# Norming delta-rule and attention outputs tile by tile, inside their loops, in a two-layer hybrid block

## The chip, the cores and the metric

The kernel runs on one core of a Trainium2 chip. The metric is the device time of one execution in microseconds (us). Engines are named PE (TensorE, matrix products), DVE (VectorE), ACT (ScalarE), POOL (GpSimd) and SP (SyncE, which here only issues transfers).

## The reference

Two layers work on 256 latent and 256 context tokens of width 1024. Each layer modulates its normed input, projects it with one wide matrix, runs three branches over the projections, gates and merges the three and applies a feed-forward part (a dense one in layer 0, eight experts with two per token in layer 1). In layer 1 only the latent tokens are needed after the branches, so its outputs are half as wide.

```python
# branch a: gated delta rule in chunks, both directions, 4 heads x 128
o = _rmsnorm(o.transpose(0, 2, 1, 3), gn) * jax.nn.silu(z.reshape(bsz, n, HA, DVA))
# branch b: gated linear attention in chunks, both directions, 4 heads x 128
o = _rmsnorm(o.transpose(0, 2, 1, 3), gn) * jax.nn.silu(r.reshape(bsz, n, HB, DVB))
# branch c: differential attention, 4 heads: softmax(q1 k1) - lam * softmax(q2 k2), times v
o = _rmsnorm(o, gn) * (1.0 - lam_init)
# merge of the three
(ga * (ya @ w_o_a) + gb * (yb @ w_o_b) + gd * (yd @ w_o_c)) @ w_out
```

Each branch's output is divided by its root mean square over the 128 values of a head and token, so a token's norm needs that token alone. The mean is over one head: heads are independent.

## The kernel before

**Layout.** A branch's output oT lies as 128 head values on the partitions by head by token: `oT[:, h, t]` (512 tokens in layer 0, 256 in layer 1). The sum of squares over the partitions is a matmul with a matrix of ones, which leaves the sum on every partition.

**Products.** A float32 projection is done as three matmuls (mm3, L272 to L274) of operands that are split in a high part (ACT copy, L267) and a rest (DVE subtraction, L268). Weights stream through three buffers named raw, filled from SP's queue in the order in which they are written.

**Order of work.** PLAN lists the stages of a layer: pr and iv prepare the delta rule's chunks and invert their triangular matrices, sc is `a_scan`, gla the linear attention, dif the `diff` attention, ha, hb and hc are `head_out` of the branches, ma, mb and mc their merges. "m16" asks for 16 units of the modulation matrices (w_mod; L348, a load of 1 MB and eight matmuls each, four units to a group), "ga4" for gate projections ahead of time, "za" for z's projection ahead of time, stored in DRAM and read again later. Within the program a list scheduler of the programming layer decides each engine's order: it lets later work run ahead of earlier work where that waits. Tiles of a pool, though, are handed out in the program's order. PSUM tiles come from two such pools, `pm` (tag "mm", 3 tiles: projections, modulation, merges, norms) and `pq` (tag "q", 5 tiles: the steps of scan and attention). Each engine then executes its list in order.

**The chains.** `a_scan` (L730) takes four steps, in each the two directions; a step's 128 tokens go through w (L746), V (L759, L761), sp (L767) and o (L781, L782), and the state S is carried to the next step. In the order table `[[0, 1, 2, 3], [1, 0, 3, 2]]` a tile of tokens is written by one direction (copy, L784) and completed by the other in an odd step (addition, L786). `diff` (L1039) takes query tiles of 128 tokens and in each the heads in turn: products pq (L1052), maximum (L1053), exponential (L1056), combination (L1061, L1062), transposes tp (L1065), copy PT (L1067) and products oc (L1069); after the four heads oc is copied to oT.

**The outputs.** `head_out` (L825) norms a branch's finished oT head by head over all its tokens: square (ACT, L842), ones matmul (L844), the inverse root (`rstd`, two ACT steps, L407), multiplications (DVE), split. For branch a it reads the stored z back whole into a raw buffer (`fetch`, L232).

Of the kernel before, what the change touches and what calls it, by code (L numbers as in the profile page):

```python
# [13 lines left out]
AF = mybir.ActivationFunctionType  # L14
OP = mybir.AluOpType
# [9 lines left out]
MOE_PART = 3  # L25
PRE = (7,)
PLAN = ("sm ap su pr iv ga4 m4 za sc m16 dec qkB gb1 ha ma vB gla qC kC m4 gc1 vC hb dif mb hc mc",
        "sm ap pr ga1 m8 iv sc za m6 ga3 m1 gc1 qkB dec vB ha ma gla qC kC m1 vC hb dif mb hc mc")
MOE_PRE = 9
MOE_AT = 0  # L30
PART = 512
# [165 lines left out]
class Prog:  # L197
# [532 lines left out]
    def a_scan(self, l, s):  # L730
        nc, D, T = self.nc, self.D, self.T
        t0 = 2 * l
        oT = self.ch([4, 512 - 256 * l], "oTa")
        mm = nc.tensor.matmul
        bc = lambda n, d, tt: D[n][:, d, tt][:, :, None].to_broadcast([128, 4, 128])
        S = [None, None]
        wT = {}
        order = [[0, 1, 2, 3], [1, 0, 3, 2]]

        def wt(i, d):  # L740
            tt = order[d][i]
            X = self.sm([4, 128], "Xs")
            nc.vector.tensor_mul(X, s["U"][d][:, 4 * tt:4 * tt + 4], bc("negc", d, tt))
            p = self.pq((4, 128), "w")
            for h in range(4):
                mm(p[:, h], s["k"][:, tt, h], X[:, h], start=True, stop=True)  # L746
            wT[d] = self.sm([4, 128], "wT")
            nc.scalar.copy(wT[d], p)

        for i in range(4):  # L750
            for d in range(2):
                tt = order[d][i]
                out = tt >= t0
                qs = slice((tt - t0) * 128, (tt - t0 + 1) * 128)
                if i:
                    wt(i, d)
                V = self.pq((4, 128), "V")
                for h in range(4):
                    mm(V[:, h], s["U"][d][:, 4 * tt + h], s["v"][:, tt, h], start=True, stop=not i)  # L759
                    if i:  # L760
                        mm(V[:, h], wT[d][:, h], S[d][:, h], start=False, stop=True)  # L761
                if i < 3:
                    vk = self.sm([4, 128], "vk")
                    nc.vector.tensor_mul(vk, V, bc("bk", d, tt))
                    sp = self.pq((4, 128), "sp")
                    for h in range(4):
                        mm(sp[:, h], s["k"][:, tt, h], vk[:, h], start=True, stop=True)  # L767
                if out:
                    vn = self.sm([4, 128], "vn")
                    nc.vector.tensor_mul(vn, V, bc("beta", d, tt))  # L770
                    if l:
                        qe = T["q"][:, 1 - d, :, qs]
                    elif i:
                        R = self.a_rows(d, tt)
                        qe = self.sm([4, 128], "qe")
                        nc.scalar.activation(qe, R, AF.Exp)
                        nc.vector.tensor_mul(qe, qe, T["q"][:, :, qs])
                    o = self.pq((4, 128), "o")
                    for h in range(4):
                        if i:  # L780
                            mm(o[:, h], S[d][:, h], qe[:, h], start=True, stop=False)  # L781
                        mm(o[:, h], vn[:, h], s["AT"][d][:, tt - t0, h], start=not i, stop=True)  # L782
                    if i % 2 == 0:
                        nc.scalar.copy(oT[:, :, qs], o)  # L784
                    else:
                        nc.vector.tensor_add(oT[:, :, qs], oT[:, :, qs], o)  # L786
                if i < 3:
                    Sn = self.sm([4, 128], "S")
                    if not i:
                        nc.scalar.copy(Sn, sp)  # L790
                    else:
                        for h in range(4):
                            nc.vector.scalar_tensor_tensor(Sn[:, h], S[d][:, h], D["egl"][:, d, tt, h:h + 1],
                                                           sp[:, h], op0=OP.mult, op1=OP.add)
                    S[d] = Sn
        return oT
# [14 lines left out]
    def gates_ahead(self, l, j, H, count):  # L811
# [5 lines left out]
        for _ in range(count):  # L817
            pr = len(done)
            done.append(pr)
            for c, p in enumerate(self.proj(l, U_G + 3 * pr + j, H, 256 * l)):  # L820
                s = self.sd([512], "sg")[:, :n]
                self.sigmoid(s, p)
                self.nc.scalar.dma_start(g[pr // 2][:, 2 * (pr % 2) + c], s)

    def head_out(self, l, oT, gn, H, u, name):  # L825

        nc = self.nc
        c0 = 256 * l
        n = 512 - c0
        zs = self.stashed.get((l, "z" + name))  # L830
        if l == 0:
            yh = self.ch([4, 512], "yh", F32R)
            yl = self.ch([4, 512], "yl", F32R)
        else:
            y = self.ch([2, 4, 256], "yhl", F32R)
            yh, yl = y[:, 0], y[:, 1]
        for h in range(4):
            o = oT[:, h]
            if zs is None and u is not None and h % 2 == 0:
                pz = self.proj(l, u + h // 2, H, c0)  # L840
            sq = self.sd([512], "sq")
            nc.scalar.activation(sq[:, :n], o, AF.Square)  # L842
            ps = self.pm()
            nc.tensor.matmul(ps[:, :n], self.ones, sq[:, :n], start=True, stop=True)  # L844
            if zs is not None:
                rs = self.rstd(ps[:, :n], n, 1.0 / 128)
                if h == 0:
                    z = self.fetch(zs)
                nc.vector.tensor_mul(o, o, rs[:, :n])
                nc.vector.tensor_mul(o, o, z[:, h])  # L850
            elif u is None:
                rs = self.rstd(ps[:, :n], n, 1.0 / 128)
                nc.vector.scalar_tensor_tensor(o, o, gn, rs[:, :n], op0=OP.mult, op1=OP.mult)
            else:

                pv = next(pz)
                z = self.sd([512], "z")
                nc.scalar.activation(z[:, :n], pv, AF.Exp, scale=-1.0)
                nc.vector.scalar_tensor_tensor(o, o, gn, pv, op0=OP.mult, op1=OP.mult)
                nc.scalar.activation(z[:, :n], z[:, :n], AF.Ln, bias=self.one)  # L860
                nc.scalar.activation(sq[:, :n], ps[:, :n], AF.Ln, bias=self.eps, scale=1.0 / 128)
                nc.vector.scalar_tensor_tensor(z[:, :n], sq[:, :n], 0.5, z[:, :n], op0=OP.mult, op1=OP.add)
                nc.scalar.activation(z[:, :n], z[:, :n], AF.Exp, scale=-1.0)
                nc.vector.tensor_mul(o, o, z[:, :n])
            self.split(yh[:, h], yl[:, h], o)
        if self.dbg is not None and f"{name}{l}" in self.dbg:
            nc.sync.dma_start(self.dbg[f"{name}{l}"][:, :, c0:512], oT)
        return yh, yl
# [170 lines left out]
    def diff(self, l, q, k, vC):  # L1039
        nc = self.nc  # L1040
        mm = nc.tensor.matmul
        oT = self.ch([4, 512 - 256 * l], "oTc")
        for qt in range(2 * l, 4):
            nk = 256 if qt < 2 else 512
            cs = slice((qt - 2 * l) * 128, (qt - 2 * l + 1) * 128)
            o = self.pq((4, 128), "oc")
            for h in range(4):
                E, r = [], self.ti([4], "r")
                for m in range(2):
                    ms = slice(64 * m, 64 * m + 64)  # L1050
                    p = self.pq()
# [16 lines left out]
                for j in range(nk // 128):  # L1068
                    mm(o[:, h], vC[:, j, h * 128:(h + 1) * 128], PT[:, j], start=j == 0, stop=j == nk // 128 - 1)  # L1069
            nc.scalar.copy(oT[:, :, cs], o)  # L1070
        return oT


# [499 lines left out]
```

## Time and profile before

| | |
|---|---|
| median of 3 runs | 2604.29 us |
| lowest and highest | 2601.22 and 2613.67 us |
| profiled execution | 2607.5 us, its span 2605.7 us |
| mean granted PE clock | 0.962 |
| PE busy | 2455.8 us (94% of the span) |
| DVE busy | 1718.3 us (66%) |
| ACT busy | 1417.3 us (54%) |
| HBM traffic | 181 GB/s over the span |

The profiled execution is a run of its own, so its times are compared with it and not with the median. A busy engine may be busy with work that could stand elsewhere; what sets a stage's length is read from that stage's windows and waits. In all times of the trace 0 is the start of the span.

### The profile page before, as it was taken

The numbers are of one execution on the slowest core, as the hardware profiler recorded it, in microseconds if no ns is written. First come the engines' busy times: TensorE is split into PE (matmuls) and PEld (weight loads), VectorE is DVE, ScalarE is ACT, GpSimd is POOL, SyncE is SP. The second block draws the span as 40 slices with busy tenths as digits, with TensorE's granted clock in tenths as the row PEclk, the third lists the DMA queues.
The fourth block names the chain that finished last, engine by engine and source line by source line (L and its number), as shares of the span: only waits on it lengthen the run. The fifth ranks groups of instructions, "written<-read, shape, count | busy, mean of one in ns | idle before, by whom it ended". The sixth has DMA issues, their size and how long they took to land.

```text
span 2605.7 us, 35872 instructions
## 1 busy us (share of the span) xinstructions
PE 2455.8 (94%) x13712; PEld 1979.8 (76%) x13712; DVE 1718.3 (66%) x3130; ACT 1417.3 (54%) x2352; POOL 87.6 (3%) x216
## 2 busy tenths in 40 slices
PE   5998999999998999998979999998999999999997
PEld 3786777677677788886859878787878888878876
DVE  4675446655644533335686475767988888988987
ACT  3764343225553432334845432666878777777775
POOL 0000001110010000000000010010000000000000
PEclk8998999989999999998978999998999999999998
DMA  6323632022132223222273130246979899999994
GB/s 248 110 93 149 246 132 71 17 106 81 49 128 83 81 77 121 96 74 89 97 271 115 46 141 33 89 169 261 386 270 365 332 350 351 346 347 353 342 366 181
DMA packets 72707, 473.13 MB, mean 182 GB/s; under 512 B 8208, under 2 KB 10384, under 8 KB 19664
## 3 DMA queue, kind: packets, MB, share of 16 engines
q1 hardware_dynamic: 68208, 464.73, 48.1%
q10 hardware_dynamic: 4320, 6.03, 0.6%
q8 instruction: 110, 1.80, 0.3%
q14 instruction: 69, 0.57, 0.1%
HBM read 463.65 MB, written 7.08 MB: 181 GB/s over the span
## 4 chain that ended last, share of the span: by engine, by line
PE 85%; DVE 8%; ACT 4%; issue 2%; DMA 1%; SPq 0%; POOL 0%; ACTq 0%; DVEq 0%; POOLq 0%
PE pm L273 19%; PE pm L272 19%; PE pm L274 19%; PE y L274 3%; PE y L273 3%; PE y L272 3%; PE la L985 2%; PE pm L348 2%; PE pq L1052 1%; DVE ATb L987 1%; PE pm L844 1%; PE ob L996 1%; PE tp L1352 1%; DMA raw<-in_wmod_dram 1%; DVE zq L973 1%
## 5 line engine op out<-in xcount | busy, mean ns | idle before, releaser
L268 DVE TENSOR_TENSOR whl<-raw,whl 128x512 fp32r<-128x512 f32 (+2 forms) x490 | 331.2, 682 | 341.0 <-ACT whl L267 338.0
L272 PE MATMUL pm<-hh,whl 128*128 128x512 f32 (+2 forms) x1264 | 477.7, 380 | 13.0 <-ACT whl L267 6.6
L274 PE MATMUL pm<-hh,whl 128*128 128x512 f32 (+2 forms) x1264 | 467.7, 371 | 12.3 <-DVE whl L268 12.3
L267 ACT CAST whl<-raw 128x512 fp32r<-128x512 f32 (+2 forms) x490 | 289.8, 600 | 339.9 <-PE pm L274 268.7
L273 PE MATMUL pm<-hl,whl 128*128 128x512 f32 (+2 forms) x1264 | 470.9, 373 | 0.0
L268 DVE TENSOR_TENSOR wp<-rawc,wp 128x1024 fp32r<-128x1024 f32 x261 | 313.6, 1222 | 36.7 <-ACT wp L267 30.6
L272 PEld LDWEIGHTS pm<-hh,whl 128*128 128x128 f32 (+1 forms) x1264 | 244.8, 194 | 60.6 <-ACT whl L267 8.6
L274 PEld LDWEIGHTS pm<-hh,whl 128*128 128x128 f32 (+1 forms) x1264 | 243.5, 193 | 54.8 <-DVE whl L268 14.3
L267 ACT CAST wp<-rawc 128x1024 fp32r<-128x1024 f32 x261 | 268.1, 1051 | 21.1 <-PE y L274 11.5
L273 PEld LDWEIGHTS pm<-hl,whl 128*128 128x128 f32 (+1 forms) x1264 | 244.7, 194 | 42.6 <-issue 6.3
L268 DVE TENSOR_TENSOR wlo<-raw,whi 128x1024 fp32r<-128x1024 f32 x176 | 210.0, 1222 | 34.1 <-ACT whi L267 31.6
L273 PE MATMUL pm<-wlo,hg 128*128 128x512 f32 x530 | 211.8, 400 | 1.6 <-DVE wlo L268 1.4
L272 PE MATMUL pm<-whi,hg 128*128 128x512 f32 x530 | 211.2, 398 | 0.0
L274 PE MATMUL pm<-whi,hg 128*128 128x512 f32 x530 | 207.7, 392 | 0.0
L267 ACT CAST whi<-raw 128x1024 fp32r<-128x1024 f32 x176 | 179.0, 1052 | 13.2 <-PE pm L273 11.9
L273 PE MATMUL y<-wp,mt 128*128 128x512 f32 x348 | 135.4, 389 | 0.0
L274 PE MATMUL y<-wp,mt 128*128 128x512 f32 x348 | 135.3, 389 | 0.0
L273 PEld LDWEIGHTS pm<-wlo,hg 128*128 128x128 f32 x530 | 99.7, 188 | 34.6 <-DVE wlo L268 15.8
L272 PE MATMUL y<-wp,mt 128*128 128x512 f32 x348 | 120.1, 389 | 0.2 <-ACT mt L1354 0.2
L272 PEld LDWEIGHTS pm<-whi,hg 128*128 128x128 f32 x530 | 99.7, 188 | 20.9 <-ACT hg L1328 0.2
L274 PEld LDWEIGHTS pm<-whi,hg 128*128 128x128 f32 x530 | 99.7, 188 | 20.2
L268 DVE TENSOR_TENSOR wlo<-rawc,whi 128x1024 fp32r<-128x1024 f32 x91 | 110.9, 1219 | 1.9 <-ACT whi L267 1.3
(394 smaller groups left out, 4542.8 us busy)
## 6 DMA issues: line engine op xcount, KB each, us to landing
rawc<-in_m_dram SPq DMA_DIRECT2D x176, 1024.0 KB, 6.0
raw<-in_m_dram SPq DMA_DIRECT2D x88, 1024.0 KB, 7.4
raw<-in_win_dram SPq DMA_DIRECT2D x64, 1024.0 KB, 4.9
raw<-in_wmod_dram SPq DMA_DIRECT2D x40, 1024.0 KB, 5.0
raw<-in_f_dram SPq DMA_DIRECT2D x22, 1024.0 KB, 4.8
raw<-in_wo_dram SPq DMA_DIRECT2D x24, 512.0 KB, 3.7
raw<-in_f_dram SPq DMA_DIRECT2D x16, 704.0 KB, 4.0
rawc<-in_wmod_dram SPq DMA_DIRECT2D x8, 1024.0 KB, 16.9
```

What stands on the lines that cost most here:

```text
L267: self.nc.scalar.copy(hi, src)
L268: self.nc.vector.tensor_sub(lo, src, hi.bitcast(F32))
L272: mm(p, wh, ah, start=first, stop=False)
L273: mm(p, wh, al, start=False, stop=False)
L274: mm(p, wl, ah, start=False, stop=last)
L348: nc.tensor.matmul(p[j:j + 32, :256], self.cs[:, k, o:o + 32], w[:, k], start=i == 0 and k < 4, stop=i == n - 1 and k >= 4)
L844: nc.tensor.matmul(ps[:, :n], self.ones, sq[:, :n], start=True, stop=True)
L973: nc.vector.tensor_mul(FQ[hp][r, x, a].rearrange("p (n s) -> p n s", s=LEVELS[li]), side(Fj[:, x]), side(q[hp]))
L985: mm(p[:, x % 2, hp], FK[hp][:, x], FQ[hp][:, x], start=True, stop=True)
L987: nc.vector.copy_predicated(AT.rearrange("p h a (n t s) -> p (h a) n t s", t=2, s=s)[:, :, :, 1 - d], mk[:, None].to_broadcast([128, 4, 64 ...
L996: mm(o[:, hp], vB[:, tt, h * 128:(h + 1) * 128], AT[:, hp, a], start=True, stop=first)
L1052: mm(p[:, :nk], q[ms, h, cs], k[ms, h, :nk], start=True, stop=True)
```

## The change

A function `head_tile` norms one tile of 128 tokens for all four heads: one square, one ones matmul of 512 columns, one inverse root, and either two multiplications (branch a, the second by a tile of z that is fetched on SP) or one that also applies the gain (branch c). `a_scan` calls it when a tile's second direction has been added (four tiles in layer 0, two in layer 1), `diff` after each query tile's copy (four and two). `head_out` of a and c then only splits; branch b is as before. In layer 1's plan za moves ahead of the scan, since the scan now reads the stored z. The z read is four transfers of 256 KB in layer 0 and two in layer 1, in place of one of 1 MB (half a MB) into a raw buffer.

```diff
--- before.py
+++ after.py
@@ -25,7 +25,7 @@
 MOE_PART = 3
 PRE = (7,)
 PLAN = ("sm ap su pr iv ga4 m4 za sc m16 dec qkB gb1 ha ma vB gla qC kC m4 gc1 vC hb dif mb hc mc",
-        "sm ap pr ga1 m8 iv sc za m6 ga3 m1 gc1 qkB dec vB ha ma gla qC kC m1 vC hb dif mb hc mc")
+        "sm ap pr ga1 m8 iv za sc m6 ga3 m1 gc1 qkB dec vB ha ma gla qC kC m1 vC hb dif mb hc mc")
 MOE_PRE = 9
 MOE_AT = 0
 PART = 512
@@ -784,6 +784,7 @@
                         nc.scalar.copy(oT[:, :, qs], o)
                     else:
                         nc.vector.tensor_add(oT[:, :, qs], oT[:, :, qs], o)
+                        self.head_tile(l, oT, self.P(f"gna{l}"), "a", qs)
                 if i < 3:
                     Sn = self.sm([4, 128], "S")
                     if not i:
@@ -822,6 +823,23 @@
                 self.sigmoid(s, p)
                 self.nc.scalar.dma_start(g[pr // 2][:, 2 * (pr % 2) + c], s)
 
+    def head_tile(self, l, oT, gn, name, cs):
+
+        nc = self.nc
+        o = oT[:, :, cs]
+        sq = self.sd([4, 128], "sq")
+        nc.scalar.activation(sq, o, AF.Square)
+        ps = self.pm((4, 128))
+        nc.tensor.matmul(ps, self.ones, sq, start=True, stop=True)
+        rs = self.rstd(ps.rearrange("p a b -> p (a b)"), 512, 1.0 / 128).rearrange("p (a b) -> p a b", a=4)
+        if name == "a":
+            z = self.sm([4, 128], "z")
+            nc.sync.dma_start(z, self.stashed[l, "za"][:, :, cs])
+            nc.vector.tensor_mul(o, o, rs)
+            nc.vector.tensor_mul(o, o, z)
+        else:
+            nc.vector.scalar_tensor_tensor(o, o, gn, rs, op0=OP.mult, op1=OP.mult)
+
     def head_out(self, l, oT, gn, H, u, name):
 
         nc = self.nc
@@ -836,6 +854,9 @@
             yh, yl = y[:, 0], y[:, 1]
         for h in range(4):
             o = oT[:, h]
+            if name != "b":
+                self.split(yh[:, h], yl[:, h], o)
+                continue
             if zs is None and u is not None and h % 2 == 0:
                 pz = self.proj(l, u + h // 2, H, c0)
             sq = self.sd([512], "sq")
@@ -1068,6 +1089,7 @@
                 for j in range(nk // 128):
                     mm(o[:, h], vC[:, j, h * 128:(h + 1) * 128], PT[:, j], start=j == 0, stop=j == nk // 128 - 1)
             nc.scalar.copy(oT[:, :, cs], o)
+            self.head_tile(l, oT, self.A["gnc", l], "c", cs)
         return oT
 
 
```

The next rows are one piece of the difference of PE's order (before: -, after: +), in the middle of layer 0's scan. V, sp, R and o are the scan's own tiles; L348 is a modulation matmul, which belongs to no step of the scan.

```order
 L759 MATMUL V<-vtok,U_951 128x128
 L761 MATMUL V<-S,wT 128x128
-L348 MATMUL pm<-raw,cs 32x256 x8
 L767 MATMUL sp<-vk,ktok 128x128 x4
 L573 MATMUL R<-cstt,gc 128x128 x4
-L348 MATMUL pm<-raw,cs 32x256 x11
 L781 MATMUL o<-qe,S 128x128
 L782 MATMUL o<-AT_955,vn 128x128
```

The modulation matmuls between the scan's steps are gone from here. Where they stand now is the end of the scan, PE's order of the changed kernel (L833 is the norm's matmul in `head_tile`, L915 belongs to the decays of branch b, L272 is the first matmul of qkB, the projection that follows).

```order
L781 MATMUL o<-qe,S 128x128
L782 MATMUL o<-AT_955,vn 128x128
L915 MATMUL pq<-w2t,smt 128x512 x2
L833 MATMUL pm<-sq,ones 128x512
L348 MATMUL pm<-raw,cs 32x256 x24
L915 MATMUL pq<-w2t,smt 128x512 x2
L348 MATMUL pm<-raw,cs 32x256 x8
L359 MATMUL pm<-cstt,modr 128x8 x2
L348 MATMUL pm<-raw,cs 32x256 x32
L272 MATMUL pm<-hh,whl 128x512
```

All 128 of them (two more runs of 32, each with its L359, lie between the last two rows) now follow the last norm of the scan. On SP the same place reads, as a piece of the difference (w_mod is the modulation matrix, za the stored z, w_in the wide projection):

```order
 L248 DMA raw<-in_win_dram 128x2048 x2
-L248 DMA raw<-in_wmod_dram 128x2048 x16
+L248 DMA raw<-in_wmod_dram 128x2048 x3
+L837 DMA z<-za_1917 128x4x128 x4
+L248 DMA raw<-in_wmod_dram 128x2048 x13
 L248 DMA raw<-in_win_dram 128x2048 x3
```

The four reads of z stand behind the third of 16 modulation loads. In layer 0's attention PE's order before, between two transposes of its last two query tiles, has projections and merge matmuls (L272 to L274):

```order
L1065 MATMUL tp<-cstt,e 128x128 x4
L1052 MATMUL pq<-kC,qC 128x512 x2
L1069 MATMUL oc<-PT,vC 128x128 x4
L272 MATMUL pm<-hh,whl 128x512
L273 MATMUL pm<-hl,whl 128x512
L274 MATMUL pm<-hh,whl 128x512
```

and eight more of these three before the next tp. After, the end of the same attention reads:

```order
L1086 MATMUL tp<-cstt,e 128x128 x4
L1073 MATMUL pq<-kC,qC 128x512
L1090 MATMUL oc<-PT,vC 128x128 x4
L1073 MATMUL pq<-kC,qC 128x512
L1086 MATMUL tp<-cstt,e 128x128 x4
L1090 MATMUL oc<-PT,vC 128x128 x4
L833 MATMUL pm<-sq,ones 128x512
L272 MATMUL pm<-yh,whl 128x512
```

The matmuls of merge b, which stood between the attention's steps, now begin behind its last norm.

## Rows read from the trace of the kernel before

**Rows 1.** The page: engines' busy time, and the chain that ended last, by engine.

```profile
PE 2455.8 (94%) x13712; PEld 1979.8 (76%) x13712; DVE 1718.3 (66%) x3130; ACT 1417.3 (54%) x2352; POOL 87.6 (3%) x216
...
PE 85%; DVE 8%; ACT 4%; issue 2%; DMA 1%; SPq 0%; POOL 0%; ACTq 0%; DVEq 0%; POOLq 0%
```

**Rows 2.** Windows of scan 0, attention 0, scan 1: engines' busy us, clock, DMA.

```profile
246.35:308.00 61.65, 60.88 (x599) 48.01 (x601) 24.82 (x54) 13.67 (x24) 0.00 (x0) 1.00 0.63 234
...
605.40:722.50 117.10, 111.23 (x516) 78.45 (x516) 73.83 (x176) 66.41 (x150) 9.32 (x6) 1.00 0.18 63
...
1399.50:1450.00 50.50, 50.50 (x420) 47.58 (x419) 24.35 (x48) 17.99 (x37) 0.00 (x0) 1.00 0.26 85
```

**Rows 3.** The window of layer 0's scan, instructions of L348 alone.

```profile
246.35:308.00 61.65, 18.51 (x242) 7.19 (x246) 1.00 0.63 234
```

**Rows 4.** DMA: modulation loads issued in that scan; rate of 0 to 40 us.

```profile
raw<-in_wmod_dram SPq DMA_DIRECT2D x13, 1024.0 KB, 4.9
...
GB/s 0 30 209 365 422 426 401 426 451 426 410 418 451 418 418 426 451 410 418 418 426 434 418 418 410 451 401 426 418 426 434 369 434 442 353 355 18 0 0 0
```

**Rows 5.** PE timeline: qkB's first matmul; late modulation loads of layer 1.

```profile
314.81 0.80 PE L272 MATMUL pm<-hh,whl 128*128 128x512 f32 x1
...
1322.45 1.07 PE L348 MATMUL pm<-raw,cs 128*32 128x256 f32 x16 [1.12 <-DMA raw<-in_wmod_dram]
1325.62 1.94 PE L348 MATMUL pm<-raw,cs 128*32 128x256 f32 x16 [2.10 <-DMA raw<-in_wmod_dram]
```

**Rows 6.** PE timeline: filler in attention 0, its transposes, filler in attention 1.

```profile
657.67 0.40 PE L272 MATMUL pm<-yh,whl 128*128 128x512 f32 x1
...
660.40 0.39 PE L272 MATMUL pm<-yh,whl 128*128 128x512 f32 x1
...
669.65 0.66 PE L1065 MATMUL tp<-cstt,e 128*128 128x128 f32 x4 [0.32 <-DVE e L1062]
...
719.48 0.60 PE L1065 MATMUL tp<-cstt,e 128*128 128x128 f32 x4
...
1680.65 0.28 PE L272 MATMUL pm<-hh,whl 128*128 128x256 f32 x1
...
1683.89 0.28 PE L272 MATMUL pm<-hh,whl 128*128 128x256 f32 x1
```

**Rows 7.** Groups of attention 0 by line: xcount, busy us, mean ns, idle before.

```profile
L268 DVE TENSOR_TENSOR whl<-raw,whl 128x512 fp32r<-128x512 f32 x25 | 19.3, 774 | 4.0 <-ACT whl L267 3.8
...
L1056 ACT ACTIVATE e<-pq,r 128x512 f32<-128x512 f32 x16 | 11.0, 689 | 13.4 <-DVE r L1054 13.3
```

**Rows 8.** Norm matmuls at heads a0, c0, a1, c1: busy, mean ns, idle.

```profile
L844 PE MATMUL pm<-sq,ones 128*128 128x512 f32 x8 | 5.3, 746 | 2.7 <-ACT sq L842 2.7
...
L844 PE MATMUL pm<-sq,ones 128*128 128x512 f32 x8 | 5.8, 814 | 5.1 <-ACT sq L842 5.1
...
L844 PE MATMUL pm<-sq,ones 128*128 128x256 f32 x8 | 2.6, 404 | 1.3 <-ACT sq L842 1.3
...
L844 PE MATMUL pm<-sq,ones 128*128 128x256 f32 x8 | 3.3, 499 | 3.6 <-ACT sq L842 3.6
```

**Rows 9.** Windows of 4 us: PE's busy time and the granted clock (PEclk).

```profile
528.00:532.00 4.00, 3.02 (x23) 1.82 (x21) 1.88 (x3) 0.00 (x0) 0.00 (x0) 1.00 1.01 426
532.00:536.00 4.00, 4.00 (x22) 2.84 (x21) 0.35 (x1) 1.72 (x5) 0.29 (x2) 0.72 0.32 133
...
728.00:732.00 4.00, 1.51 (x4) 0.30 (x2) 2.12 (x3) 3.04 (x6) 0.00 (x0) 0.97 0.88 350
732.00:736.00 4.00, 2.70 (x4) 0.91 (x4) 1.44 (x2) 1.87 (x4) 0.00 (x0) 0.50 0.99 418
```

**Rows 10.** DVE timeline in layer 1's inverse.

```profile
1357.87 0.17 DVE L366 TENSOR_TENSOR mod<-pm,par 128x8 f32<-128x8 f32 x1 [2.10 <-PE pm L359]
...
1370.88 0.18 DVE L655 TENSOR_TENSOR W<-W,fs 128x31 f32<-128x31 f32 x1
...
1374.77 2.12 DVE L658 COPY_PREDICATED W<-mk,W 128x1024 f32<-128x1024 uint8 x1 [0.26 <-ACT W L657]
```

## The prediction

> **What bounds the kernel now.** I read the page's first part and its chain of waits first: TensorE (PE) is busy 94% of the span and carries 85% of the chain that ended last [rows 1]. So PE idles 150 us in all, and a change that removes small waits can win only part of that; a change that creates idle time on PE loses all of it. Next I read the windows of the three chains that the change enters, the scan of the delta rule and the attention of both layers [rows 2]. Each is a chain of short steps between PE, VectorE (DVE) and ScalarE (ACT), yet PE is busy 60.88 of 61.65 us in layer 0's scan and 111.23 of 117.1 in its attention. The reader should see that the chain does not supply this: in the scan 18.51 us are L348, modulation matmuls that belong to other work [rows 3], and in the attention most of it is L272 to L274, projections and merges. This other work (filler) runs in the gaps of the chain. The question is what the change does to it.
>
> **The change part by part.** The order lists show that the filler goes. A norm's matmul takes a slot of the same three PSUM tiles ("mm") that all filler uses, and slots are given in program order, so work written after the chain cannot run before the norm inside it. Counted in the lists: in layer 0's scan 117 modulation matmuls fall to none, in layer 0's attention 297 filler matmuls (L272 to L274) to 72, in layer 1's scan 128 to none, in its attention 303 to 72. None is removed: all come later, when no chain is there to fill. I sum stage by stage, first with PE at full clock.
>
> A, layer 0's scan to qkB. The chain's own steps remain, so I keep its 62 us: the filler put between its steps goes (about -3), the norm tiles put between them cost about 1 each (+4: four norms keep PE busy 5.3 [rows 8], 1.3 each, and the next step's DVE work waits behind a norm's multiplies). Then all 16 modulation loads' matmuls run after it. Three loads are in the raw buffers; the other 13 MB can only start as buffers come free, after the scan, and now nothing hides them. In the scan they were free: 13 issues, 4.9 us each to land [rows 4]. Back to back, a MB costs 2.5 us at the 421 GB/s of the kernel's first 40 us [rows 4] (1.05 MB over it), and with these three buffers 3.2 in layer 1, where units that wait for their load start at 1322.45 and 1325.62 [rows 5]. I take 2.7. qkB's weights are the fourteenth load: 309.5 + 4.9 + 13 x 2.7 + 1.3 for their split gives 350.8, against 314.81 now [rows 5]: +36 (33 to 42 for 2.5 to 3.2).
>
> B, branch a's output in layer 0: four norms there cost 5.3 us busy and 2.7 idle [rows 8]; they go, but the linear attention that starts beside them loses that cover (I take +3): -5.
>
> C, layer 0's attention, merge b, output c. The lost filler is 297 - 72 = 225 matmuls. Twelve of them take 2.73 us [rows 6], 0.2275 each: 51 us, now after the attention. The attention itself cannot shorten by as much, since it already waits on its own chain: per head two exponentials of 0.69, as many reductions and more between two transposes (tp, L1065); tp starts at 669.65 and, seven heads later, at 719.48, 7.1 us a head [rows 6, 7]. Without the filler its DVE and ACT no longer serve 25 weight splits [rows 7] between these steps; I estimate 0.4 a head, -6. Output c's four norms cost 5.8 busy and 5.1 idle [rows 8]; the last tile's norm still stands at the end: -10. Together +35.
>
> The other tiles' norms in the attention (a square, two table steps and a multiply, some 0.7 each like the 512-column steps of [rows 7]) lie beside the next tile's chain; were each of them on it, that would be some 3 a tile, 9 in layer 0 and 3 in layer 1, and I keep that as a bound of C and F.
>
> D, layer 1's inverse and scan. There za moves ahead of the scan, and gate projections and modulation that ran beside the inverse and in the scan come after it: 243 matmuls of 256 columns at 0.12 (27 of them in 3.24 us [rows 6]) = 29, 7 modulation units of 1.07 = 7.5, and I take 8 for waits on three of their loads [rows 5]. The inverse's chain on DVE gets free of them: a modulation wait of 2.1, six splits of some 0.75 put between its steps, and 3.9 from its last short step to L658 [rows 10], -10.5, and the scan loses the steps put between its own, -4. That gives +30.
>
> E, output a of layer 1: 2.6 busy and 1.3 idle go [rows 8], -4.
>
> F, layer 1's attention: 231 x 0.12 = 28 later, four norms of 3.3 + 3.6 gone [rows 8] and 1 us besides, 4 from fewer splits: +16.
>
> The z reads become four small transfers of the same bytes on SP. They stand among the modulation loads and the later ones wait for slots until the scan is near its end, so they hold back the fourth to sixteenth load; but those wait for buffers that the scan frees no sooner, so on SP I cost this at nothing. Were the buffers free, it would be the delay of A. On DVE a norm's multiply by z waits for its transfer, and behind it stand the next step's vk and vn, for which PE waits. If a z is as late as a weight load takes, that is 4.9 [rows 4] for each of the two that are asked for late; they are asked for while the norm is still being made, so I take nothing and keep up to +10 in A's bound. POOL's queue is not touched.
>
> At full clock: 36 - 5 + 35 + 30 - 4 + 16 = +108.
>
> **The clock.** The granted clock shows 2.4 GHz or 1.2 GHz, with values between where a window holds both. At 528 to 532 PE was busy 3.02 of 4 us, and at 532 to 536 the mean was 0.72; at 728 to 732 it was busy 1.51, then 0.50 [rows 9]. In the first case PE had not stopped, it had only become sparse. With its filler gone, the attention leaves PE (117.1 less its 67 of filler is 44 of 111.23) busy some 40%, and layer 0's scan 42.4 of 62 (69%). So I expect 1.2 GHz in the attention and part of the time in the scans. PE work on the chain then doubles: about 2.3 us a 512-key head (a pq and four tp) and 1.2 a 256-key head, of which 8 and 6 remain in layer 0: +26; 7 of layer 1's heads: +16. Layer 0's scan: PE's own 42.4 would take 84.8, at most +23 over 62 (up to +36 with its latencies); I take half of the upper bound, +18. Layer 1's: own 35 in 46 us, at most +24, half +12. Sum +72.
>
> The Trainium skill, "TensorE: Matmul & The Clock Gate", section "HAM oscillation — how this bites in real kernels", says that waits of PE re-throttle it, and shows it for one long idle stretch before each burst. By the letter of that rule the chains, whose gaps are short, would keep 2.4 GHz and the sum would stay +108; the rows at 532 and 732 speak for the fall after merely sparse work, and by them it is +180. The same page's section "A second HAM failure mode: psum-queue depth-cycling" tells of frequent small idles doing the same, which agrees with the row at 532.
>
> **Sum.** The profiled execution took 2607.5 us around a span of 2605.7, 3.2 above the median of 2604.3. 2607.5 + 108 + 72 = 2787.5; less 3.2, about 2784 on the median's scale.
>
> **Rivals.** (1) Full clock is kept, only the cover is lost: 2607.5 + 108 - 3.2 = 2712. For it: PE held 2.4 GHz through all the windows of [rows 2], though filled; against it the falls of [rows 9]. (2) Both scans fall to 1.2 GHz throughout and loads take 3.2 us: 18 + 12 + 6 more, 2820. For it: the fall after the row at 528 followed work no sparser than the scans' own; against it: at the low clock PE would be busy through most of the scan, and the low clock of [rows 9] came only behind sparse work. (3) The other side: the filler, not the chain, sets the length of the attention and scan. Then they shrink to their own PE work when it goes, total PE work is unchanged, and only the norms' idle time (2.7 + 5.1 + 1.3 + 3.6 [rows 8]) leaves: 2604 - 13 = 2591. It decides only if a head's 7.1 us falls to about 4 (PE's own part is some 3.3), and the loads of A still cost 36 unless they hide as well; tp waits for DVE even with the filler in place [rows 6], which speaks against it. (4) The change gains and loses nothing that counts, because the displaced filler finds another gap of PE: of 150 idle us only what lies behind the attention could take it, and the merge waits for it there: 2604.
>
> **How the numbers follow.** Chances: forecast (2760 to 2805) 0.54, rival 1 (2705 to 2735) 0.26, rival 2 0.14, rival 3 0.03, rival 4 0.03. The range takes in the first three with their bounds: 2705 (A at 33, rest of 1) to 2830. A measurement of this kernel can tell about 0.5%, 13 us, from no change. Slower is the first three, 0.94; rival 4 is within 0.5%; rival 3 lies at -0.5%, so its 0.03 is mostly faster.
>
> **What would show it.** In the profile after: no L348 between the first L759 and the last L782 of layer 0; 13 modulation loads after it, with PE idle on DMA and qkB near 350 (or, at lower clock, 370) on the old axis; attention windows with PE under half busy and a granted clock of 0.5, then a solid block of merge b, 240 matmuls; the norm stalls of [rows 8] gone. The prediction is wrong if the granted clock stays 1.00 in the attention (then 2712), if heads come quicker than 6 us, or if qkB starts before 340.

## The result, and the profile after

The changed kernel takes 2804.8 us (median of 4 runs, 2801.9 to 2810.8) against 2603.7 before: a ratio of 1.0772, 95% interval 1.0751 to 1.0793, 7.7% slower, 201 us. Forecast were 2784 and a range of 2705 to 2830. The profiled execution of the changed kernel took 2810.8 us, 203 more than that of before.

The page's first part and its chain, as in [rows 1]: PE is busy 90% of the span, no longer 94%, and the chain that ended last holds more of DVE, ACT and DMA.

```profile
PE 2531.5 (90%) x13704; PEld 2015.9 (72%) x13704; DVE 1718.8 (61%) x3124; ACT 1420.8 (51%) x2340; POOL 88.7 (3%) x216
...
PE 81%; DVE 9%; ACT 5%; DMA 3%; issue 2%; POOL 0%; SPq 0%; DVEq 0%; ACTq 0%; POOLq 0%
```

PE runs 13704 matmuls instead of 13712 and yet shows 76 us more busy time: its matmuls take longer. Where, the windows tell. These are, in order, layer 0's scan, the stretch from its end to qkB, layer 0's attention, and scan and attention of layer 1 (length; PE, PEld, DVE, ACT and POOL busy; PEclk, DMA share, GB/s), to be held against [rows 2]:

```profile
244.80:308.00 63.20, 45.87 (x351) 40.83 (x349) 27.52 (x52) 18.34 (x30) 0.00 (x0) 0.99 0.07 22
308.00:363.70 55.70, 37.71 (x284) 14.63 (x284) 10.84 (x22) 13.51 (x25) 0.00 (x0) 0.62 0.79 284
654.70:800.30 145.60, 99.79 (x293) 55.81 (x292) 58.18 (x155) 51.82 (x122) 0.00 (x0) 0.62 0.07 26
...
1509.70:1565.20 55.50, 44.01 (x282) 37.91 (x280) 18.75 (x39) 9.46 (x18) 0.00 (x0) 0.88 0.04 10
...
1793.60:1881.30 87.70, 60.84 (x209) 35.34 (x208) 36.49 (x90) 31.30 (x74) 0.00 (x0) 0.63 0.09 30
```

The scan takes 63.2 us with PE busy 45.87, where before it took 61.65 with PE busy 60.88: it carries no filler any more. The same window with L348 alone, against 18.51 us in [rows 3]:

```profile
244.80:308.00 63.20, 0.00 (x0) 0.00 (x0) 0.99 0.07 22
```

The attention of layer 0 takes 145.6 us at a mean granted clock of 0.62 (117.1 at 1.00 before), that of layer 1 87.7 at 0.63.

Where the modulation matmuls went, PE's timeline shows (start, duration, then idle time before and what ended it), with the SP row of their loads and the median us from issue to landing:

```profile
308.34 3.78 PE L915 MATMUL pq<-w2t,smt 32*128 32x512 f32 x4
312.05 2.08 PE L833 MATMUL pm<-sq,ones 128*128 128x512 f32 x2
314.06 4.33 PE L348 MATMUL pm<-raw,cs 128*32 128x256 f32 x48
...
320.88 1.07 PE L348 MATMUL pm<-raw,cs 128*32 128x256 f32 x16 [0.59 <-DMA raw<-in_wmod_dram]
...
331.06 1.94 PE L348 MATMUL pm<-raw,cs 128*32 128x256 f32 x16 [2.10 <-DMA raw<-in_wmod_dram]
...
360.41 1.94 PE L348 MATMUL pm<-raw,cs 128*32 128x256 f32 x16 [3.91 <-DMA raw<-in_wmod_dram]
...
363.71 0.77 PE L272 MATMUL pm<-hh,whl 128*128 128x512 f32 x1
...
316.05 36.84 SPq L248 DMA_DIRECT2D raw<-in_wmod_dram  x13
...
raw<-in_wmod_dram SPq DMA_DIRECT2D x13, 1024.0 KB, 7.5
```

The three units that were in their buffers start only at 314.06, behind a decay matmul and the scan's last norm; the 13 other loads are issued from 316.05 on, and PE waits for nearly each of them. The twelve steps from the unit at 320.88 to the one at 360.41 average 3.3 us, most units take 1.9 to 1.94 instead of 1.07, a load lands 7.5 us after its issue (4.9 in [rows 4]), and qkB starts at 363.71 (314.81 in [rows 5]).

In layer 0's attention the timeline reads, over one head of 512 keys, with the first and the last transposes of the eight such heads around it:

```profile
724.47 1.11 PE L1086 MATMUL tp<-cstt,e 128*128 128x128 f32 x4 [1.36 <-DVE e L1083]
...
744.96 1.12 PE L1086 MATMUL tp<-cstt,e 128*128 128x128 f32 x4 [3.36 <-DVE e L1083]
746.01 2.07 PE L1073 MATMUL pq<-kC,qC 64*128 64x512 f32 x2
748.01 2.08 PE L1090 MATMUL oc<-PT,vC 128*128 128x128 f32 x8
750.01 2.07 PE L1073 MATMUL pq<-kC,qC 64*128 64x512 f32 x2
755.50 1.11 PE L1086 MATMUL tp<-cstt,e 128*128 128x128 f32 x4 [3.42 <-DVE e L1083]
...
796.76 1.11 PE L1086 MATMUL tp<-cstt,e 128*128 128x128 f32 x4 [3.42 <-DVE e L1083]
```

The same products in the trace of before:

```profile
712.75 1.12 PE L1052 MATMUL pq<-kC,qC 64*128 64x512 f32 x2
713.80 1.16 PE L1069 MATMUL oc<-PT,vC 128*128 128x128 f32 x8
```

From tp to tp this head takes 10.5 us; on average over the seven steps from 724.47 to 796.76 it is 10.3, where [rows 6] has 7.1. A pq takes 2.07 instead of 1.12, oc 2.08 instead of 1.16, and no L272 stands in the 3.4 us in which PE waits for DVE.

By stages, from the starts of the same instructions in both traces (us):

| stage | before | after | difference |
|---|---|---|---|
| layer 0: the scan's first V to qkB | 68.5 | 118.9 | +50 |
| from there to the attention | 290.6 | 291.0 | 0 |
| the attention | 116.3 | 145.5 | +29 |
| from its end to the output projection | 69.9 | 113.1 | +43 |
| from there to layer 1's scan | 607.9 | 596.3 | -12 |
| layer 1: the scan | 50.0 | 55.5 | +6 |
| from its end to the linear attention | 66.0 | 111.4 | +45 |
| from there to the attention | 115.9 | 117.1 | +1 |
| the attention | 68.6 | 87.7 | +19 |
| from its end to the output projection | 44.4 | 68.0 | +24 |

These sum to 205, and the rest of the kernel is as before.

### The profile page after: what moved, and what is told of

It reads as the page before. It is cut to its first block, busy times and chain, and to the rows that moved or that the text cites. A ratio compares the mean times of both kernels' runs of the same rounds, so it can differ in the third digit from the quotient of the medians.

```text
span 2808.8 us, 35911 instructions
## 1 busy us (share of the span) xinstructions
PE 2531.5 (90%) x13704; PEld 2015.9 (72%) x13704; DVE 1718.8 (61%) x3124; ACT 1420.8 (51%) x2340; POOL 88.7 (3%) x216
## 4 chain that ended last, share of the span: by engine, by line
PE 81%; DVE 9%; ACT 5%; DMA 3%; issue 2%; POOL 0%; SPq 0%; DVEq 0%; ACTq 0%; POOLq 0%
PE pm L273 18%; PE pm L272 18%; PE pm L274 18%; PE y L274 3%; PE y L273 3%; PE y L272 3%; PE pq L1073 2%; DMA raw<-in_wmod_dram 2%; PE la L1006 2%; PE oc L1090 1%; PE pm L348 1%; DVE ATb L1008 1%; PE ob L1017 1%; DVE whl L268 1%; DVE zq L994 1%
## 5 line engine op out<-in xcount | busy, mean ns | idle before, releaser
L272 PE MATMUL pm<-hh,whl 128*128 128x512 f32 (+2 forms) x1264 | 475.7, 378 | 12.7 <-ACT whl L267 8.3
L274 PE MATMUL pm<-hh,whl 128*128 128x512 f32 (+2 forms) x1264 | 467.0, 370 | 7.3 <-DVE whl L268 7.3
L272 PEld LDWEIGHTS pm<-hh,whl 128*128 128x128 f32 (+1 forms) x1264 | 243.6, 193 | 56.2 <-ACT whl L267 10.1
L274 PEld LDWEIGHTS pm<-hh,whl 128*128 128x128 f32 (+1 forms) x1264 | 242.1, 192 | 48.2 <-DVE whl L268 9.8
L272 PE MATMUL pm<-whi,hg 128*128 128x512 f32 x530 | 210.8, 398 | 0.0
L274 PE MATMUL pm<-whi,hg 128*128 128x512 f32 x530 | 207.6, 392 | 0.0
L274 PE MATMUL y<-wp,mt 128*128 128x512 f32 x348 | 135.3, 389 | 0.0
L272 PE MATMUL y<-wp,mt 128*128 128x512 f32 x348 | 120.1, 389 | 0.2 <-ACT mt L1376 0.2
L272 PEld LDWEIGHTS pm<-whi,hg 128*128 128x128 f32 x530 | 99.5, 188 | 20.8
L274 PEld LDWEIGHTS pm<-whi,hg 128*128 128x128 f32 x530 | 99.6, 188 | 20.1
```

The costliest lines, as they stand in the source:

```text
L272: mm(p, wh, ah, start=first, stop=False)
L274: mm(p, wl, ah, start=False, stop=last)
```

## The experiments

Theory A is the prediction's: what counts is where the norms stand in the order in which tiles are handed out, ahead of the filler; the filler then runs after the chains, and the chains without it run at the low clock. Rival B: the norms' own steps, between the steps of the chains, cost the time.

**1. The norms' tiles from the chain's own pools.** The norms stay where the change puts them.

```diff
-        sq = self.sd([4, 128], "sq")
+        sq = self.sm([4, 128], "sq")
-        ps = self.pm((4, 128))
+        ps = self.pq((4, 128))
-        rs = self.rstd(ps.rearrange("p a b -> p (a b)"), 512, 1.0 / 128).rearrange("p (a b) -> p a b", a=4)
+        rs = self.sm([4, 128], "rs")
+        nc.scalar.activation(rs, ps, AF.Ln, bias=self.eps, scale=1.0 / 128)
+        nc.scalar.activation(rs, rs, AF.Exp, bias=self.zero, scale=-0.5)
```

> Same norms at the same places as in the changed kernel, but their three tiles come from the pools that the chain itself uses (PSUM from pq, square and root from the pool of the steps), so that the filler need not wait for their slots. In PE's order the filler is back: 128 modulation matmuls in layer 0's scan and 312 filler matmuls in its attention, where the changed kernel has 0 and 72. Theory A (the loss comes from filler that slots in program order keep out of the chains, and the low clock follows from that): 2585 to 2610 us, granted clock back to 0.96. Rival B (the loss comes from the norms' own steps, standing between the steps of the chains on ACT and DVE, and from the z reads): at least 2750 us.

Measured: 2617.7 us, 1.0064 of before (1.0045 to 1.0082), clock 0.967. Of the 201 us 187 are gone, with every norm in its early place: theory A holds and B falls, though the time lies above A's range. The windows of the two attentions:

```profile
606.80:735.00 128.20, 117.56 (x532) 81.79 (x532) 77.21 (x183) 73.27 (x160) 12.98 (x8) 0.98 0.23 83
1638.40:1714.90 76.50, 73.06 (x484) 58.56 (x484) 53.31 (x118) 51.77 (x120) 6.17 (x7) 1.00 0.27 94
```

PE is busy 117.56 of 128.2 us there at 0.98, but the stage is 12 us longer than before (15 more filler matmuls stand in it, and what follows is 6 us shorter). One place shows a part of it:

```profile
696.62 0.66 PE L1088 MATMUL tp<-cstt,e 128*128 128x128 f32 x4
...
700.83 1.13 PE L833 MATMUL pq<-sq,ones 128*128 128x512 f32 x2
701.89 1.13 PE L1075 MATMUL pq<-kC,qC 64*128 64x512 f32 x4
...
708.16 0.63 PE L1088 MATMUL tp<-cstt,e 128*128 128x128 f32 x4 [0.59 <-DVE e L1085]
```

The norm's matmul, whose tile now comes ahead of the next query tile's in the chain's pool, stands before that tile's first pq; this head takes 11.5 us from tp to tp, its neighbours 7.8 and 7.7.

**2 and 3. One branch alone.** The attention's outputs by tile with branch a and the plan as before; then the reverse (with the plan's swap). The first line is of the first run, the last of the second; the lines that make `head_out` and the plan fit are left out.

```diff
-                        self.head_tile(l, oT, self.P(f"gna{l}"), "a", qs)
...
-            self.head_tile(l, oT, self.A["gnc", l], "c", cs)
```

> Only the attention's outputs are normed by tile; branch a and the plan are as before. Stage by stage, the profile of the changed kernel puts about 72 us on layer 0's attention with its merges and 43 us on layer 1's. Theory A: the parts add, 2604 + 115 = about 2719 us, the attention of both layers at 1.2 GHz. If the low clock in the attention needed the stages ahead of it to be late too: nearer to 2604 + 115 - 42 = 2677 us.

> Only the delta rule's outputs are normed by tile, with za ahead of the scan in layer 1; the attention is as before. The profile of the changed kernel puts 50 us on layer 0's scan with its modulation loads and about 43 us on layer 1's scan and what follows. Theory A: 2604 + 93 = about 2697 us, and together with the run of the attention's part alone the sum of the two losses is that of the whole, 201 us within 15.

Measured: 2719.1 us (1.0444, 1.0427 to 1.0462) and 2692.2 us (1.0337, 1.0320 to 1.0355). The losses of 115 and 88 us sum to 204, that of the whole is 201. The attention is as slow alone, so its low clock is its own:

```profile
604.90:750.20 145.30, 99.50 (x292) 55.74 (x292) 58.16 (x155) 51.78 (x122) 0.00 (x0) 0.62 0.07 26
```

**4. The norm by tile, asked for at the old place.**

```diff
+        if name != "b":
+            for t in range(4 - 2 * l):
+                self.head_tile(l, oT, gn, name, slice(t * 128, (t + 1) * 128))
```

> Norms by tile of 128 tokens for all four heads, as in the changed kernel, but all asked for where the whole output is normed in the kernel before, and the plan as before; only the form of the norm differs from before. PE's order has all its filler (117 modulation matmuls in the scan, 297 in the attention). Theory A: 2604 us within 15. Rival B (the tile form itself is dearer, by its narrower steps and four z reads): at least 2630 us.

Measured: 2611.5 us, 1.0031 (1.0009 to 1.0053). The form of the norm costs at most some 0.5%.

**5. Useless matmuls in the attention.** The changed kernel with work added on PE alone.

```diff
+                tf = tp.rearrange("p a b -> p (a b)")
+                for x, n in ((E[0], nk), (E[1], nk), (E[1], 256)):
+                    mm(tf[:, :n], self.C("ident"), x[:, :n], start=True, stop=True)
```

> The changed kernel with three useless matmuls a head in the attention (the two exponentials times the identity, 512, 512 and 256 columns at 512 keys), written into the PSUM tile that the transposes overwrite afterwards. They add work on PE and no work elsewhere, and the filler stays displaced. Theory A (of the attention's longer stay, 145.5 and 87.7 us against 116.3 and 68.6 before, the greater part is PE at 1.2 GHz on the chain's own matmuls): granted clock back to 1.00 there, layer 0's attention down to about 124 us, layer 1's to about 72, the kernel about 37 us faster than the changed one, 2768 us. Rival B (the chain's length does not hang on PE's clock, only filler was displaced): the attention no shorter, each head up to 2.6 us longer, 2805 to 2840 us.

Measured: 2774.2 us, 1.0662 (1.0639 to 1.0685): 31 us faster than the changed kernel, by doing more. The two attentions; 10 us in the heads of 256 keys of layer 0's; and transposes of its eight heads of 512 keys, the first, two in the middle and the last:

```profile
644.10:779.20 135.10, 118.90 (x389) 67.07 (x388) 59.02 (x155) 50.72 (x122) 0.00 (x0) 0.81 0.08 28
1767.10:1836.40 69.30, 62.63 (x257) 35.31 (x256) 36.40 (x90) 30.65 (x74) 0.00 (x0) 0.93 0.11 38
...
680.00:690.00 10.00, 9.54 (x22) 5.44 (x22) 3.02 (x11) 1.30 (x5) 0.00 (x0) 0.50 0.00 0
...
729.10 0.60 PE L1089 MATMUL tp<-cstt,e 128*128 128x128 f32 x4
...
744.30 0.60 PE L1089 MATMUL tp<-cstt,e 128*128 128x128 f32 x4
...
750.28 0.60 PE L1089 MATMUL tp<-cstt,e 128*128 128x128 f32 x4
...
776.92 0.65 PE L1089 MATMUL tp<-cstt,e 128*128 128x128 f32 x4
```

Layer 1's attention is at 0.93 and takes 69.3 us instead of 87.7. Layer 0's is 135.1 long at 0.81, which is the low clock for 51 us of it. Its heads of 512 keys run at full clock; from 729.10 to 776.92 they take 6.8 us each on average (6.0 in the pair shown), against 10.3 in the changed kernel. So the low clock costs some 3.5 us a head, and A's reading of the clock holds there.

The 124 us expected for layer 0 were not reached, mostly because the clock did not come back in the heads of 256 keys: at 680 to 690 PE is busy 9.54 of 10 us, and the granted clock is still 0.50. The useless matmuls only lengthen these heads, to 7.6 us on average from 6.2 in the changed kernel.

**6. The norm's PSUM tile alone from pq.** Of the edit in 1 only this:

```diff
-        ps = self.pm((4, 128))
+        ps = self.pq((4, 128))
```

> The changed kernel with the norm's PSUM tile alone taken from pq; its square and its root stay in the pool that filler's sigmoids and modulation rows use. PE's order has some of the filler back: 32 of 128 modulation matmuls in layer 0's scan, none in layer 1's, 156 and 132 filler matmuls in the attentions (72 and 72 in the changed kernel, 297 and 303 before). If the loss goes with the count of displaced filler: 37 + 43 + 45 + 32 = 157 of the 201 us stay, about 2760 us. If the PSUM slots alone were the cause: 2620 us or less.

Measured: 2772.6 us, 1.0655 (1.0630 to 1.0679): 168 of the 201 us stay, 11 more than the count of filler gave. So the PSUM slots alone are not the cause; the pool of square and root, which the sigmoids and modulation rows use too, holds filler back in the same way. (With that pool alone changed and the PSUM tile left in pm, PE's order has no more filler than the changed kernel's, 0 in the scan and 72 in the attention; this was not run.) The attention of layer 0:

```profile
634.50:783.80 149.30, 105.89 (x376) 65.36 (x376) 63.79 (x164) 56.48 (x129) 2.94 (x2) 0.74 0.11 39
```

84 more filler matmuls stand in it than in the changed kernel, and at 0.74 it is 149.3 us long; they shorten the merges behind it (96.6 us to the output projection instead of 113.1) and not the attention.

**7. The norms asked for right behind the loops.**

```diff
-                        self.head_tile(l, oT, self.P(f"gna{l}"), "a", qs)
+        for t in range(4 - t0):
+            self.head_tile(l, oT, self.P(f"gna{l}"), "a", slice(t * 128, (t + 1) * 128))
```

(and likewise in the attention)

> The norms by tile are asked for right behind the loops of scan and attention instead of inside them, and ahead of all the work that served as filler; the plan is that of the changed kernel. So no step of a norm is written between the chain's steps, but the slots are still taken before the filler's; PE's order has as little filler as the changed kernel (0 and 0 in the scans, 72 and 72 in the attentions). Theory A (the place in the order of slots counts): 2790 to 2815 us. Rival B (the norms' steps inside the chains): 2700 us or less.

Measured: 2797.0 us, 1.0739 (1.0721 to 1.0757). Nothing of the norm is written between the chains' steps, and the loss is nearly whole: the order against the filler decides, not the loop. Layer 0's scan, and what follows it up to qkB:

```profile
244.60:303.70 59.10, 44.40 (x348) 39.80 (x347) 25.69 (x49) 16.30 (x27) 0.00 (x0) 1.00 0.08 23
303.70:356.00 52.30, 35.98 (x288) 14.79 (x287) 12.37 (x25) 15.22 (x28) 0.00 (x0) 0.67 0.81 302
```

The scan takes 59.1 us, so the norms inside it cost 4 us in the changed kernel, as the prediction's A took, and the stretch behind it still takes 52.3.

**8. z's reads from ACT's queue.**

```diff
-            nc.sync.dma_start(z, self.stashed[l, "za"][:, :, cs])
+            nc.scalar.dma_start(z, self.stashed[l, "za"][:, :, cs])
```

> The changed kernel with z's reads issued by ACT instead of SP, so that nothing stands between the third and the fourth modulation load on SP. The prediction costs the four reads on SP at nothing, since the fourth load waits for a buffer that only PE's first modulation matmuls free, after the scan: the loads start no earlier, 2805 us within 6, qkB at 363 us within 2. Rival: the reads hold the loads back, and without them qkB starts at least 6 us earlier.

Measured: 2802.4 us, 1.0766 (1.0747 to 1.0785), the changed kernel's time. On SP, then on PE:

```profile
315.60 37.38 SPq L248 DMA_DIRECT2D raw<-in_wmod_dram  x13
...
362.10 0.79 PE L272 MATMUL pm<-hh,whl 128*128 128x512 f32 x1
```

With nothing ahead of them on SP the loads are issued 0.45 us earlier and qkB starts 1.6 earlier: the four reads cost what the prediction took, about nothing.

**9 and 10. Towards a faster version.** From the kernel of 1: the attention's norm two heads later; and the early norm for the delta rule alone.

```diff
+                if h == 2 and qt > 2 * l:
+                    self.head_tile(l, oT, self.A["gnc", l], "c", late)
```

> The kernel with the norms' tiles from the chain's pools, but in the attention a tile's norm is written two heads later, inside the next query tile (the last one at the end). In the trace of the undeferred one the norm's matmul stands ahead of the next tile's first pq, and the head at a tile's border takes 9.9 to 12.2 us where its neighbours take 6 to 9. Theory A: the four borders (three in layer 0, one in layer 1) lose about 3.5 us each, 2617 - 14 = about 2604 us, no better than the kernel before. If the norm's steps cost the chain as much wherever they stand: 2617 us.

> The norms' tiles from the chain's pools, for the delta rule alone; the attention's outputs as in the kernel before. Its stages in the run with both parts: layer 0 level with before at the end of the linear attention (583.7 us both), layer 1's scan to the attention's start 236.8 us against 231.9. Theory A: 2604 + 5 = about 2609 us; the early norm gains nothing there even with all filler in place. If the idle time of the four norms that goes (2.7 + 1.3 us) were a gain: 2600 us.

Measured: 2621.3 us (1.0056, 1.0040 to 1.0072) and 2614.4 (1.0030, 1.0016 to 1.0044). The first expectation failed: the slow head moved from the border into the tile (10.1 and 11.5 us in layer 0), and nothing came back. The second lies a little above its own. None of these early norms beats the kernel before.

**11. The order by the plan alone.** The changed kernel with "za m16 sc" in layer 0 and the gates and modulation of layer 1 ahead of sc.

```diff
-iv ga4 m4 za sc m16 dec
+iv ga4 m4 za m16 sc dec
-iv za sc m6 ga3 m1 gc1 qkB
+iv za m6 ga3 m1 gc1 sc qkB
```

> The changed kernel with its plan alone edited: the modulation units and the gate projections that ran behind the scans are asked for ahead of them, so their slots come before the norms' slots; pools, norms and attention are as in the changed kernel. In PE's order 104 of 128 modulation matmuls are back in layer 0's scan, nearly all in its first half, and layer 1's scan has none (its gates run beside the inverse). Theory A (order of slots): of the changed kernel's 93 us for branch a some 60 come back, 2745 us; layer 0 reaches qkB near 325 to 335 instead of 363.7 and layer 1's scan-to-linear-attention part stays 10 to 20 longer than before. Rival (the norms in the scan cost this themselves): 2790 us or more.

Measured: 2768.8 us, 1.0615 (1.0587 to 1.0643). 36 of the 60 us expected come back, with pools and norms untouched, which is A's direction, and not its size. In layer 1 the stretch from the scan's first V to the linear attention's first la takes 130.8 us, 10 more than before, as expected (171.7 in the changed kernel). Layer 0 misses what was expected: the scan is longer than I took it to be, since PE now waits for the loads in its first half (one such wait is shown), and qkB starts at 344.77:

```profile
251.70:339.50 87.80, 66.11 (x578) 50.32 (x574) 31.28 (x67) 20.98 (x37) 0.00 (x0) 0.93 0.58 218
...
288.64 1.93 PE L348 MATMUL pm<-raw,cs 128*32 128x256 f32 x16 [1.91 <-DMA raw<-in_wmod_dram]
...
344.77 0.50 PE L272 MATMUL pm<-hh,whl 128*128 128x512 f32 x1
```

## Why the prediction was right, point by point

**The mechanism** was right: the filler is displaced (L348 in the scan 18.51 to 0 us), comes back behind the chains, and the attention falls to the low clock. Experiments 1, 4, 7 and 11 show that it is the order of the norms against the filler, 2 and 3 that the parts add, 5 that the clock is a cause of its own. But the prediction named one pool, the three PSUM tiles; experiment 6 shows that a second one holds filler back as well. By stages the forecast of +180 is 25 under the measured 205: the terms of C and F are each 11 too small, and A's comes near by luck.

**A**, +36 and +18 for the clock: 54, measured 50, by other parts. The scan did not fall to the low clock: it ran at 0.99, with PE busy 45.87 of 63.2. The step "part of the time in the scans" failed there. In its place the loads after the scan were late and slow. On the axis of before (the changed kernel's scan starts 1.6 us earlier) they were issued at 317.6 instead of 309.5, since the modulation matmuls stand behind the decay and the norm on PE, and they came 3.3 us apart instead of 2.7: 8 + 13 x 0.6 = 16 us, about the 14.5 by which qkB, at 365.3 on that axis, is later than the 350.8 of the sum at full clock. Whether the 3.3 comes from the clock of that stretch (0.62, a unit takes 1.94 us before its buffer is free) or from the loads themselves (7.5 us to land) no run separates.

**B**, -5: measured 0. That the cover which the linear attention lost took back what the norms gave would fit, but is not shown.

**C**, +35 and +26: 61, measured 72. The merges' share is +43, close to the 51 - 10; the attention grew by 29, not 20. The term that was too small is the clock's: 2.3 us a head was taken for one pq and the tp. From one tp to the next the timeline has the tp, both pq and the oc, which take 0.5, twice 0.95 and 0.9 us longer than before, 3.3 in all; a head takes 10.3 us, 3.2 more than before and 3.5 more than at the full clock of experiment 5. The relief from the weight splits, 0.4 a head, is about right: 7.1 us with filler, 6.8 without it at full clock, there with the useless matmuls. The sign "PE under half busy" did not come: as its matmuls take longer, PE is busy 99.79 of 145.6 us.

**D and E**, +30, +12 and -4: 38, measured 40. The stretch up to the scan, with the inverse in it, won 12 where 10.5 were forecast; the scan ran at 0.88 and lost 6 where I took 8.

**F**, +16 and +16: 32, measured 43: by the same clock term +19 in the attention for 16 - 4, and +24 behind it for 28 - 7.

**The rivals.** Full clock throughout (2712) is excluded by the attentions' 0.62 and 0.63. The low clock throughout both scans is excluded by 0.99 and 0.88, but that rival's price of a load, 3.2 us, was the better one, and at 2820 it lies nearer to the measured 2805 than the forecast does. The other side needed heads of some 4 us; those of 512 keys took 10.3, and 6.8 at full clock without filler. Its gain, the norms' idle time, does not come even with the filler in place: experiments 1, 9 and 10 have it there, and none wins.

The step that failed is the clock in layer 0's scan. These are the longest waits of PE in the changed kernel's first scan, first attention and second scan, and the window behind the last one:

```profile
305.76 0.46 PE L781 MATMUL o<-qe,S 128*128 128x128 f32 x2 [2.48 <-DVE qe L777]
...
684.65 0.69 PE L1086 MATMUL tp<-cstt,e 128*128 128x128 f32 x2 [4.77 <-DVE e L1083]
...
1522.92 2.04 PE L746 MATMUL w<-Xs,ktok 128*128 128x128 f32 x8 [1.98 <-DVE Xs L743]
...
1522.20:1528.90 6.70, 5.69 (x24) 5.27 (x24) 0.57 (x1) 0.59 (x1) 0.00 (x0) 0.50 0.00 0
```

The Trainium skill, "TensorE: Matmul & The Clock Gate", section "HAM oscillation — how this bites in real kernels", has waits of PE re-throttle it. The attention's rows agree: there PE, once the filler is gone, waits for DVE or ACT in every head, up to 4.77 us, at 0.62. For layer 0's scan, whose waits are shorter, the rule as the prediction read it gives full clock, and 0.99 was measured; the prediction had set it aside there for one row of [rows 9]. In layer 1's scan, though, no wait is longer than 1.98 us, and yet the clock was at 0.50 from the end of such a wait on (0.88 over the scan). So the rows of the two scans differ, and what makes the clock fall stays open.

## What to carry to other kernels

Where a scheduler lets later work fill the gaps of a chain, look at which pools new work takes tiles from: a tile asked for early in program order and filled late bars all later users of its pool, and the cost is the filler's, not the new work's. Price such a change by the filler that it displaces, by the loads that this filler asks for, and by the clock of what stays behind. Idle time that a norm shows at the end of a stage is no gain by itself; moved into the chain, the norms won nothing here (experiments 1, 9 and 10).

## What the runs showed of the hardware that was not expected

PE idle for about a quarter of layer 0's scan (17.3 of 63.2 us, no wait over 2.48) kept 0.99, while the attention, where PE waits up to 4.77 us, had 0.62. Adding matmuls whose results are thrown away made the kernel 31 us faster (experiment 5), but being busy did not bring the clock back at once: with PE busy 9.54 of 10 us it was still 0.50 there at 680 to 690. Filler in part did not help either: with 84 more real filler matmuls layer 0's attention stood at 0.74 and was no shorter (experiment 6).
